# GpSimd drains right behind its last gather, not at the end of the section

## The chip, the cores and the metric

The kernel runs on one core of a Trainium2 chip. The metric is the time of one execution on the device in microseconds, as the median of several executions. Each run also reports the core's span, which here is some 1.7 us shorter than the time; a profile is one recorded execution.

## The reference

An embedding lookup with a position term: 32 batches of 512 indices into a table of 50,000 rows of 512 floats, plus a position row for each place in the sequence.

```python
def reference(indices, embedding_table, position_embed):
    token_embed = embedding_table[indices]
    return (token_embed + position_embed).astype(np.float32)
```

The output is 33.5 MB, and as much is gathered from the table.

## The kernel before

All the work stands in one critical section with hand-written semaphores. GpSimd issues 128 indirect gathers of 128 rows each, VectorE adds the position term to each, and SyncE stores the result.

```python
    with tc.tile_critical():
        # ... SyncE loads the indices and position_embed ...
        for g in range(B * K):                      # 32 * 4 gathers
            # ... waits for the indices and for a free slot ...
            ins = nc.gpsimd.indirect_dma_start(
                out=slots[b % SLOTS][:, k, :], out_offset=None, in_=table,
                in_offset=bass.IndirectOffsetOnAxis(ap=where, axis=0),
            ).then_inc(s_gather[g % LANES], 16)
            if g >= LANES:
                ins._wait_ge(s_gather[g % LANES], rounds(g - LANES))
        # ... TensorE, VectorE, ScalarE ...
        for b, at, n in stores:
            # ... one store, which waits for its adds ...
        nc.sync.wait_ge(s_rest, 16 * rest)          # the last store has landed
```

When the section closes, the built program makes SyncE signal the other engines, each of which executes a drain, by which an engine finishes what it has begun, and answers; SyncE collects the answers. Then come two barriers of all five engines, in which GpSimd counts the others' arrivals and releases them, with three drains of GpSimd around them. Below, "the section's end" is the first part and "the end barrier" the second.

## Time and profile before

| | us |
|---|---|
| time, median of 3 runs | 180.75 (180.0 to 181.29) |
| the profiled execution: time, span | 184.1, 182.4 |
| last packet on the DMA queues | 174.5 |
| from there to the end of the span | 7.9 |

Read the table from the last row up: while the DMA engines are busy, the work is done; after them comes a tail of pure synchronisation. The profiled execution took 3.35 us longer than the median of the timed ones. The lines of the profile are in the prediction. In them SP is SyncE, POOL GpSimd, DVE VectorE, ACT ScalarE and PE TensorE; a q marks an engine's sequencer.

### The profile page before, as it was taken

How to read it: one execution, taken by the hardware profiler on the slowest of the kernel's cores; microseconds unless marked ns; L12 is line 12 of the kernel's file. 1: busy time of each engine (PE TensorE's matmuls, PEld its weight loads, DVE VectorE, ACT ScalarE, POOL GpSimd, SP SyncE). 2: the span in 40 equal slices, each digit the busy share in tenths (PEclk: the TensorE clock that was granted, in tenths of full speed). 3: DMA queues.
4: the chain of work that ended last, by engine and by line, in shares of the span. 5: the costliest groups of instructions: out<-in, count | busy, mean ns of one | idle time of the engine just before them, and what ended most of it. 6: DMA issues, size and time to landing. Idle time of an engine off the chain costs nothing.

```text
span 182.4 us, 398 instructions
## 1 busy us (share of the span) xinstructions
PE 0.7 (0%) x4; PEld 0.6 (0%) x4; DVE 87.1 (48%) x130; ACT 3.6 (2%) x5; POOL 121.8 (67%) x134
## 2 busy tenths in 40 slices
PE   0100000000000000000000000000000000000000
PEld 0100000000000000000000000000000000000000
DVE  0253635546545445738355644455474655454400
ACT  2500000000000000000000000000000000000000
POOL 3777777777777777777777777777777777750000
DMA  4999999999999999999999999999999999999910
GB/s 116 323 270 345 356 382 405 413 405 418 394 371 396 408 403 406 403 417 420 417 413 412 418 412 408 417 418 417 414 412 422 404 415 416 418 407 417 406 70 0
DMA packets 17634, 68.32 MB, mean 375 GB/s; under 512 B 3008, under 2 KB 3008, under 8 KB 14560
## 3 DMA queue, kind: packets, MB, share of 16 engines
q0 software_dynamic: 10240, 33.56, 48.4%
q1 hardware_dynamic: 7392, 34.74, 46.6%
q14 instruction: 2, 0.02, 0.0%
HBM read 34.74 MB, written 33.55 MB: 374 GB/s over the span
## 4 chain that ended last, share of the span: by engine, by line
POOL 63%; issue 24%; DMA 6%; DVE 1%; SPq 0%; POOLq 0%
POOL slot L121 63%; DMA slot<-in_embedding_table_dram,idx_t 5%; DVE slot L150 1%; DMA idx<-in_indices_dram 1%; POOLq L119 0%; SPq L193 0%; SPq L94 0%
## 5 line engine op out<-in xcount | busy, mean ns | idle before, releaser
L121 POOL DMA_INDIRECT slot<-in_embedding_table_dram,idx_t x124 | 117.3, 946 | 37.8 <-issue 37.8
L150 DVE TENSOR_TENSOR slot<-slot,pos_ps 128x512 f32<-128x512 f32 x128 | 86.4, 687 | 80.0 <-issue 39.3
L121 POOL DMA_INDIRECT slot<-in_embedding_table_dram,idx x4 | 4.0, 993 | 2.5 <-DMA idx<-in_indices_dram 1.6
L139 DVE CAST idx_f<-idx_raw 32x512 f32<-32x512 int32 x1 | 0.4, 415 | 4.5 <-DMA idx_raw<-in_indices_dram 4.5
L156 ACT COPY pos_ps<-pos_sb 128x512 f32<-128x512 f32 x4 | 2.3, 587 | 4.4 <-DMA pos_sb<-in_position_embed_dram 4.4
L156 ACT ACT_TABLE_LOAD x1 | 1.3, 1283 | 1.0 <-SPq L94 1.0
L133 PE MATMUL turned<-ident,idx_f 32*128 32x32 f32 x4 | 0.7, 307 | 4.9 <-DVE idx_f L139 4.9
L142 DVE CAST idx_t<-turned 128x128 int32<-128x128 f32 x1 | 0.3, 291 | 0.8 <-PE turned L133 0.8
L133 PEld LDWEIGHTS turned<-ident,idx_f 32*128 32x128 f32 x4 | 0.6, 208 | 4.9 <-DVE idx_f L139 4.9
L106 POOL MEMSET ones<- 32x32 f32 x1 | 0.1, 115 | 0.5 <-SPq L94 0.5
L182 POOL MEMSET const-float32-0.0<- 128x1 f32 x1 | 0.1, 103 | 0.3 <-issue 0.3
L107 POOL TENSOR_SCALAR_AFFINE_SELECT ident<-ones 32x32 f32<-32x32 f32 x1 | 0.2, 203 | 0.1
L182 POOL MEMSET const-uint8-127<- 128x1 uint8 x1 | 0.1, 120 | 0.0
L182 POOL MEMSET const-bfloat16-1.0<- 128x1 bf16 x1 | 0.1, 114 | 0.0
L182 POOL MEMSET const-float32-1.0<- 128x1 f32 x1 | 0.1, 106 | 0.0
## 6 DMA issues: line engine op xcount, KB each, us to landing
out_dram<-slot SPq DMA_DIRECT2D x24, 1024.0 KB
out_dram<-slot SPq DMA_DIRECT2D x10, 512.0 KB
out_dram<-slot SPq DMA_DIRECT2D x12, 256.0 KB
slot<-in_embedding_table_dram,idx_t POOLq DMA_INDIRECT x124
pos_sb<-in_position_embed_dram SPq DMA_DIRECT2D x4, 256.0 KB, 3.0
idx_raw<-in_indices_dram SPq DMA_DIRECT2D x1, 128.0 KB, 3.0
slot<-in_embedding_table_dram,idx POOLq DMA_INDIRECT x4
idx<-in_indices_dram SPq DMA_DIRECT2D x1, 4.0 KB, 1.7
```

The source lines that it names most:

```text
L106: nc.gpsimd.memset(ones[:], 1.0).then_inc(s_ident, 1)
L107: nc.gpsimd.affine_select(out=ident[:], in_=ones[:], pattern=[[-1, B]], compare_op=mybir.AluOpType.is_equal, fill=0.0, base=0, channel_mul ...
L121: ins = nc.gpsimd.indirect_dma_start(out=slots[b % SLOTS][:, k, :], out_offset=None, in_=table, in_offset=bass.IndirectOffsetOnAxis(ap=whe ...
L133: ins = nc.tensor.transpose(turned[:, k, :], idx_f[:, :, k], ident[:])
L139: nc.vector.tensor_copy(out=idx_f[:].rearrange("b p k -> b (p k)"), in_=idx_raw[:, :, 0])._wait_ge(s_raw, 16).then_inc(s_cast, 1)
L142: nc.vector.tensor_copy(out=idx_t[:], in_=turned[:])._wait_ge(s_turn, K).then_inc(s_idx, 1)
L150: nc.vector.tensor_tensor(out=part, in0=part, in1=pos_ps[k][:], op=add)._wait_ge(s_gather[g % LANES], rounds(g)).then_inc(s_add, 1)
L156: nc.scalar.copy(out=pos_ps[k][:], in_=pos_sb[k][:])._wait_ge(s_pos[k], 16).then_inc(s_ps, 1)
L182: nc = _bacc.Bacc("TRN2", target_bir_lowering=False, num_devices=1)
```

## The change

The intent: GpSimd has nothing to do after its last gather, so its drain can be worked off there, beside the last transfers, rather than in the serial tail. A flag takes GpSimd's drain out of the section's end (a nop stands in its place), and a drain is written behind the gathers. On the other engines the built program is the same.

```diff
-    with tc.tile_critical():
+    with tc.tile_critical(no_gpsimd_drain=True):
...
             if g >= LANES:
                 ins._wait_ge(s_gather[g % LANES], rounds(g - LANES))
+        nc.gpsimd.drain()
```

## The prediction

> **What bounds the kernel now.** I read four things in this order: the page for the span and the rows of slices, the stretches of the span for the end, the chain of waits, and then the instructions by source line, because the last stretch holds none that the page counts as busy. The page first:
>
> ```profile
> span 182.4 us, 398 instructions
> ...
> POOL 3777777777777777777777777777777777750000
> DMA  4999999999999999999999999999999999999910
> ```
>
> A slice is 4.56 us. The DMA engines are full from the third slice to the thirty-eighth; GpSimd (POOL) issues its last gather at 162 us; after about 174.5 us nothing moves. The stretches say it more sharply (columns: the stretch, its length, busy us and number of instructions of each engine, granted clock, DMA share, GB/s):
>
> ```profile
> 100.00:140.00 40.00, 0.00 (x0) 0.00 (x0) 21.68 (x33) 0.00 (x0) 30.25 (x33) 1.00 1.02 415
> 165.00:174.60 9.60, 0.00 (x0) 0.00 (x0) 3.44 (x6) 0.00 (x0) 0.00 (x0) 1.00 0.96 386
> 174.60:182.40 7.80, 0.00 (x0) 0.00 (x0) 0.00 (x0) 0.00 (x0) 0.00 (x0) 1.00 0.00 0
> ```
>
> Two parts, then: a body of about 174.6 us bound by DMA bandwidth (share 1.02, 415 GB/s), and a tail of 7.8 us, 4.3% of the span, in which no byte moves and no engine computes. The change can only act on the tail, or on the last 12 us of the body, where GpSimd is idle today. The chain of waits does not help: it follows back from the last busy instruction, an add on VectorE that ends at 172.3 us, and never sees the tail.
>
> ```profile
> POOL 63%; issue 24%; DMA 6%; DVE 1%; SPq 0%; POOLq 0%
> ```
>
> The tail is found by asking for the instructions of the line that opens the critical section (L94), and of the line to which the kernel's end barrier is booked (L193). Rows: line, sequencer, operation, count, duration in ns (min/median/max), first and last start in us:
>
> ```profile
> L94 SPq COMPARE_BRANCH  x1: 33/33/33, 174.9 to 174.9; - x1
> L94 SPq EVENT_SEMAPHORE  x3: 17/713/1397, 175.1 to 177.9; - x3
> L94 SPq NOP  x1: 691/691/691, 179.4 to 179.4; - x1
> L94 ACTq DRAIN  x1: 8/8/8, 175.1 to 175.1; - x1
> L94 POOLq DRAIN  x1: 2515/2515/2515, 175.1 to 175.1; - x1
> L94 DVEq DRAIN  x1: 17/17/17, 175.1 to 175.1; - x1
> L94 PEldq DRAIN  x1: 8/8/8, 175.1 to 175.1; - x1
> ```
>
> ```profile
> L193 POOLq EVENT_SEMAPHORE  x4: 17/17/17, 179.4 to 182.3; - x4
> L193 POOLq DRAIN  x3: 34/34/131, 177.7 to 180.0; - x3
> L193 SPq DRAIN  x3: 4/11/699, 180.7 to 182.2; - x3
> L193 ACTq EVENT_SEMAPHORE  x2: 17/17/17, 179.5 to 182.3; - x2
> ```
>
> SyncE sees the last store land, leaves the section (174.9) and signals the four others. All drain. Three need 8 to 17 ns; GpSimd needs 2515 ns. SyncE collects the five answers, then two barriers follow, at 179.4 and 182.2. The reader is to see that one drain is 150 times as long as any other and stands in the middle of a serial tail.
>
> **What the Trainium skill says.** "Perfetto Trace Analysis", section "Sequencer-only Instruction (DRAIN, etc)": the profiler reports only execution, from the moment the instruction's semaphores are satisfied; waiting is not in the duration. The trace agrees: GpSimd's drain starts at 175.1, with the other engines', so 2515 ns is work, not waiting. "PSUM — Partial Sum Buffer", section "Engine vs sequencer instructions": a drain waits for the engine to go fully idle, while a nop does not wait for work in flight. "VectorE: DVE Perf Modes", section "The DRAIN you can't avoid": boilerplate drains in preamble and postamble are about 12 ns on all five engines. The trace agrees for four engines and disagrees for GpSimd, which alone issued software DMAs. No page says what a GpSimd drain costs behind indirect DMAs; that the 2515 ns belong to the 128 gathers (2515/128, about 20 ns each) is my guess. Every gather had landed by 171.2 us, the end of the last packet of their queue in the trace, 3.9 us before the drain began. So the time is not waiting for data either.
>
> **The change part by part.** The built programs differ by two instructions on GpSimd and by nothing on the other engines.
>
> 1. Added: a plain drain right behind the last gather. The row of gathers puts the last start at 162.0 us and takes 0.946 us, so the drain starts at about 162.9. It has until 175.1, when SyncE signals, so 12.2 us of idle GpSimd. If it only works off finished gathers as they land, it ends just after 171.2. If it first waits for all of them and then needs its full 2.5 us, it ends at 171.2 + 2.5 = 173.7, still 1.4 us early. Cost on the path that sets the end: 0 in both cases.
> 2. Removed: the drain at the section's end. A nop takes its place, waits for the same signal, and gives the same answer. Say 0.03 us, by the small instructions around it. GpSimd then answers at about 175.15 instead of 177.64.
> 3. Kept: the three GpSimd drains of the end barrier. Today they cost 34, 131 and 34 ns, the first straight after the long one. In the changed kernel the first is again a drain with nothing issued since the last one, so I take 34 ns again.
>
> What that is worth depends on whether SyncE really waits for GpSimd. The semaphore updates in the trace say yes: GpSimd's answer is posted at 177.64 and SyncE's next step at 177.67, 0.03 us later, while the other three have answered by 175.2. Gain if SyncE is otherwise prompt: 177.64 - 175.18 = 2.46 us, so 180.75 - 2.46 = 178.3 us, or 1.4%.
>
> **The rivals.**
>
> *SyncE is slow by itself.* Its records in the tail are spaced by multiples of about 0.7 us (1397, 713, 691, 699 ns), and it still works through them until 182.2, long after GpSimd is done. If those steps are real and owe nothing to GpSimd, SyncE reaches the step that needs GpSimd late anyway: three steps of 0.7 us after 175.2 is 177.3, and the gain shrinks to about 0.4 us (180.4). Against it: the first end barrier passes at 179.4 and needs SyncE, yet SyncE's record of arriving there is stamped after 182, so its stamps lag the events and can't be taken literally. Partly for it: SyncE does arrive 1.7 us after GpSimd's answer at the first barrier, and the profiled execution took 184.1 us against 180.75 without a profile, as if the recording itself slowed it. Without recording I expect a prompt SyncE, so a larger share of the 2.46 us.
>
> *The drain's cost reappears later.* If the 2.5 us is not the gathers' bookkeeping but the price of the first drain after a long idle, the first drain of the end barrier pays it: it would run from 175.2 to 177.7, beside SyncE's steps, and hold the barrier instead. Gain 0 to 0.1 us without a profile. For it: nothing but that idle time was not varied. Against it: GpSimd's drain at the kernel's start took 193 ns.
>
> *The early drain disturbs the body.* If it keeps looking at descriptor rings while the last eight or so gathers and stores are moving, it could slow them. The section's last 12 us run at 386 to 413 GB/s; a loss of 5% there would be 0.6 us. Nothing in the profile speaks for it. If the early drain ran beyond 175.1, GpSimd would answer late again; it would have to be 4 us or longer after the last landing to lose anything.
>
> None of these makes the kernel slower by over 2% (3.6 us), and none gains 3.6 us: the whole drain is 2.5.
>
> **Range and chances.** I weigh a full gain (178.3) at 0.7, a small one (180.2) at 0.15, none (180.7) at 0.15: 0.7 x 178.3 + 0.15 x 180.2 + 0.15 x 180.7 = 178.9. The most likely value is lower than the mean; I choose 178.6. The three runs of before spread over 180.0 to 181.29, so 0.7 us either way. Low end: the full gain with a fast run, 177.5. High end: 180.5, a small gain in a usual run. Faster by over 2% needs less than 177.1 us: 0.04. Slower by over 2% needs more than 184.4: 0.01. Within 2%: 0.95.
>
> **What would show it right or wrong.** In the changed profile, step 1 is right if a GpSimd drain starts near 163 us and ends before 175 (its length should be near 8 us if it waits for landings). Step 2 is right if GpSimd shows a short nop near 175.1, and the first barrier comes about 2.4 us earlier relative to the last store. Step 3 is right if the end barrier's first GpSimd drain stays near 34 ns; a 2.5 us drain there means that the cost came back. If SyncE's 0.7 us steps fill the gap, the tail after 174.6 stays near 7.8 us although GpSimd answered early: then SyncE was the limit. If the body's end moves beyond 174.6 us by more than the usual spread, the early drain disturbed the transfers.

## The result, and the profile after

The changed kernel took 178.75 us (median of 4 runs, 178.02 to 179.02), the kernel before 180.6 us (4 runs, 180.0 to 181.29). The ratio is 0.989 with a 95% interval of 0.9843 to 0.9937: some 1% faster. A ratio here is the mean time of one kernel's fast runs over that of the other's of the same rounds, so not quite the ratio of the medians.

The changed kernel's page, the two rows that answer to those shown of before:

```profile
span 177.0 us, 399 instructions
...
POOL 4777777777777777777777777777777777776000
DMA  4989999999999999999999999999999999999993
```

The DMA row is now full up to the last slice. The empty slices at the end are gone. The stretches of the end:

```profile
165.00:175.00 10.00, 0.00 (x0) 0.00 (x0) 3.91 (x6) 0.00 (x0) 0.00 (x0) 1.00 0.93 376
175.00:177.00 2.00, 0.00 (x0) 0.00 (x0) 0.00 (x0) 0.00 (x0) 0.00 (x0) 1.00 0.00 0
```

The tail without a moving byte is 2.0 us instead of 7.8. That is 5.8 us less, far more than the drain's 2.5 us and than the 1.9 us by which the medians differ. So these two profiles must not be subtracted from each other. First the rows of the section's end and of the end barrier (which is now booked to line 194), then the early drain (line 129):

```profile
L94 SPq EVENT_SEMAPHORE  x3: 17/28/28, 175.6 to 175.9; - x3
L94 POOLq NOP  x1: 13/13/13, 175.7 to 175.7; - x1
L94 SPq NOP  x1: 13/13/13, 175.9 to 175.9; - x1
```

```profile
L194 POOLq EVENT_SEMAPHORE  x4: 17/17/17, 176.1 to 176.9; - x4
L194 POOLq DRAIN  x3: 34/41/131, 175.7 to 176.7; - x3
L194 SPq DRAIN  x3: 7/7/7, 176.0 to 176.3; - x3
```

```profile
L129 POOLq DRAIN  x1: 23301/23301/23301, 150.2 to 150.2; - x1
```

Two things have changed. GpSimd's drain is out of the tail: 23.3 us long, it ends at 173.5, and a nop of 13 ns answers in its place. And SyncE is quick: its steps take 7 to 28 ns, where in the profile of before most took 700 to 1400. The change can't be the plain cause of the second, as SyncE executes the same instructions.

The difference between the two recordings is visible in part 6 of the page, the issues with the time to landing. Before, and after:

```profile
slot<-in_embedding_table_dram,idx_t POOLq DMA_INDIRECT x124
```

```profile
slot<-in_embedding_table_dram,idx_t POOLq DMA_INDIRECT x124, 8.0
```

A landing time is printed only where the trace has all the semaphore updates of a transfer. The trace of before holds 760 updates, that of after 3384. From 40 us to 160 us, the former has 172, one per 0.70 us on average, and the latter 2003. 0.70 us is also the step that SyncE shows in the tail of before. I call the two kinds a sparse and a full recording. The experiments had to find out whether the kind belongs to the kernel or to where it runs, and what the change is worth in each.

### The profile page after: what moved, and what is told of

Its sections match the earlier page's. It is cut to its first block, busy times and chain, and to the rows that moved or that the text cites. A ratio compares the mean times of both kernels' runs of the same rounds, so it can differ in the third digit from the quotient of the medians.

```text
span 177.0 us, 399 instructions
## 1 busy us (share of the span) xinstructions
PE 0.7 (0%) x4; PEld 0.6 (0%) x4; DVE 87.7 (50%) x130; ACT 3.6 (2%) x5; POOL 122.1 (69%) x134
## 4 chain that ended last, share of the span: by engine, by line
POOL 65%; issue 25%; DMA 7%; POOLq 1%; DVE 0%; SPq 0%
POOL slot L121 65%; DMA slot<-in_embedding_table_dram,idx_t 6%; DMA idx<-in_indices_dram 1%; POOLq L129 1%; DVE slot L151 0%; SPq L194 0%; POOLq L119 0%; SPq L94 0%
```

## The experiments

### One chip, the change and its halves

Four kernels ran on one chip: the kernel before again (e1), the flag alone (e2), the early drain alone (e3), and the whole change again (e4).

```diff
 e2: flag only
-    with tc.tile_critical():
+    with tc.tile_critical(no_gpsimd_drain=True):
 e3: early drain only
+        nc.gpsimd.drain()          # behind the last gather; the section keeps its own
```

> The kernel before, unchanged, profiled a second time. All theories: GpSimd's drain at the end of the section is again about 2.5 us, and starts within 0.1 us of the other engines' drains. If SyncE's steps of 0.7 us in the tail belong to the long GpSimd drain, they come again and the profiled span is again about 182; if they were a whim of that one recording, SyncE takes under 0.1 us a step and the span is near 179, with a tail after the last store of about 4.0 us (1.5 us as in the changed kernel, plus 2.5).

> Only half of the change: the drain at the section's end is off, no drain behind the last gather. My theory (the cost is GpSimd's bookkeeping of the gathers and must be paid once, by the first drain that follows): the first drain of the end barrier takes 2.5 us in place of 0.04, starts near 175.7 and holds the first barrier; SyncE reaches that barrier 0.4 us after the section's end, so all but 0.4 us of the cost stays: ratio to before 0.998, about 180.2 us. Rival (taking the drain out of the section is what helps, the early one is decoration): ratio 0.987 to 0.989 as for the whole change.

> The other half: a drain behind the last gather, and the section's own drain kept. My theory: the early drain pays, the later one finds nothing to do and takes about 0.04 us; ratio 0.987 to 0.990, as the whole change. Rival (a drain after long idle costs 2.5 us whatever was drained before): the section's drain is 2.5 us again and the ratio is 1.00.

> The changed kernel, unchanged, in five rounds for a narrower interval and a second profile. Full gain of 2.46 us would be a ratio of 0.986; the first measurement gave 0.989. If the early drain disturbs the last gathers, the last store lands later than in the kernel before by some 0.5 us on the same chip; if not, the landing times agree within 0.3 us and the ratio tends to 0.986.

| kernel | median us | ratio to before (95%) | span of the profiled run |
|---|---|---|---|
| before (9 runs beside them) | 184.18 (184.07 to 184.33) | | |
| e1, before again | 184.2 (one look) | | 182.5 |
| e2, flag only | 184.24 | 0.9994 (0.998 to 1.0008) | 182.5 |
| e3, early drain only | 184.26 | 1.0005 (0.9991 to 1.0018) | 182.4 |
| e4, the change | 184.19 | 0.9993 (0.9979 to 1.0007) | 182.5 |

On this chip the kernel before took 184.2 us in every run, as in its first profile, and the change was worth nothing. All four recordings are sparse (754 to 770 updates). So the kind doesn't go with the kernel: the changed kernel, full in its first profile, is sparse here. Whether it goes with the chip or with the time of the run isn't shown: this was one session on one chip, and the later ones, all full, were three sessions on two other chips (the chip of the first profiles isn't on record). The rows of e4 at the section's end and of its end barrier:

```profile
L94 SPq EVENT_SEMAPHORE  x3: 17/1398/1398, 175.4 to 178.7; - x3
L94 POOLq NOP  x1: 13/13/13, 175.5 to 175.5; - x1
L94 SPq NOP  x1: 697/697/697, 180.1 to 180.1; - x1
```

```profile
L194 POOLq EVENT_SEMAPHORE  x4: 17/17/17, 180.2 to 182.4; - x4
```

GpSimd has answered at 175.5, and its early drain (22.2 us, ended at 172.8) is done. Still SyncE walks in steps of 0.7 us, the first barrier passes at 180.2 and the second near 182.3. The freed time is filled by the slow SyncE. In e1 SyncE does wait for the drain, as the prediction read it: GpSimd's answer is posted at 177.97 and SyncE's next step at 178.00. Yet the first barrier passes at 180.2 in e1 as in e4, whether the answer came early or late. In e2 the drain's 2.5 us moved into the end barrier (176.1 to 178.6), in e3 it was worked off early; neither shows in the time. In all five sparse traces, of before and of e1 to e4, the update of SyncE's arrival at the last barrier stands between 182.15 and 182.31, though SyncE left the section anywhere from 174.8 to 175.8. It is as if something held SyncE up to a fixed moment.

My expectations for e2, e3 and e4 missed the time on this chip. So did the guess in e1 that the steps of 0.7 us might belong to the long drain: e4 has them without it. What the traces show of GpSimd's drain is as expected in all three.

### The same four with the tail moved to a later time

If the hold-up ends near 182.2, a tail that starts later should be clean on any chip. The pad is four adds on VectorE, on buffers whose stores have landed, between the last landing and the section's end. The results stay correct.

```diff
-        nc.sync.wait_ge(s_rest, 16 * rest)
+        for i in range(4):
+            pad = nc.vector.tensor_tensor(
+                out=slots[8 + i][:], in0=slots[12][:], in1=slots[13][:], op=add)
+            if i == 0:
+                pad._wait_ge(s_rest, 16 * rest)
+            if i == 3:
+                pad.then_inc(s_pad, 1)
+        nc.sync.wait_ge(s_pad, 1)
```

> The kernel before with a pad: after the last store has landed, four adds of 128x2048 on VectorE (each about four times the 0.69 us of a 128x512 add, so 9 to 11 us in all), and only then the end of the section. Reason: on the last chip every kernel ended at 182.4, and in those traces only one semaphore update was recorded per 0.71 us, against a full record in the first profile of the changed kernel; SyncE stepped at the same 0.70 us until 182.2 whatever GpSimd did. Theory A (a held-up recording slows SyncE up to a fixed time near 182.2, and hides GpSimd's drain): the padded tail starts after 184 and is clean: about 0.3 + 2.5 + 1.3 us from the end of the last pad to the end of the span, GpSimd's drain 2.5 us. Theory B (SyncE is slow in every tail on such a chip, wherever it stands): the tail again takes 7 to 8 us with steps of 0.7 us. On a chip with full records both theories give the clean tail.

> The changed kernel with the same pad. Theory A: clean tail of about 1.5 us; 2.3 to 2.5 us shorter than the padded kernel before on the same chip, whichever kind of chip it is. Theory B: no difference on a chip with sparse records.

> Only the section's own drain taken out, with the pad. Theory A with the cost paid by the first later drain: the end barrier's first GpSimd drain takes 2.5 us, as it did without the pad; the end comes 0.3 to 0.5 us earlier than in the padded kernel before, not 2.4. Theory B: no difference on a chip with sparse records.

> Only the early drain added, the section's own kept, with the pad. Theory A: the section's drain takes 0.04 us, the time is within 0.1 us of the padded changed kernel. Theory B: no difference on a chip with sparse records.

| kernel, padded | median us (5 runs) | pad's end to span's end, us |
|---|---|---|
| p1, before | 189.41 (189.13 to 189.53) | 183.90 to 187.72: 3.82 |
| p2, the change | 187.04 (187.0 to 187.87) | 183.75 to 185.30: 1.55 |
| p3, flag only | 189.19 (189.09 to 189.56) | 184.08 to 187.84: 3.75 |
| p4, early drain only | 187.15 (187.04 to 187.7) | 184.00 to 185.55: 1.55 |

This was another chip, with full recordings (3386 to 3388 updates) and the kernel before at 180.73 us. So it doesn't decide between theories A and B. It does take the change apart cleanly. p1, p2, p3 and p4, the rows at the section's end (line 95 in the padded kernels) and the end barrier's drains:

```profile
L95 POOLq DRAIN  x1: 2515/2515/2515, 184.1 to 184.1; - x1
L95 SPq NOP  x1: 13/13/13, 186.7 to 186.7; - x1
```

```profile
L95 POOLq NOP  x1: 13/13/13, 184.0 to 184.0; - x1
L95 SPq NOP  x1: 13/13/13, 184.2 to 184.2; - x1
```

```profile
L95 POOLq NOP  x1: 13/13/13, 184.3 to 184.3; - x1
...
L202 POOLq DRAIN  x3: 40/123/2515, 184.4 to 187.6; - x3
```

```profile
L95 POOLq DRAIN  x1: 41/41/41, 184.2 to 184.2; - x1
```

The SPq NOP is the step that needs GpSimd's answer. In p1 it comes 2.7 us after SyncE has left the section at 183.93, right behind the drain; in p2 0.5 us after 183.78. In p3 the drain isn't gone: the first drain of the end barrier pays the full 2515 ns. So the flag alone saves 3.82 - 3.75 = 0.07 us of tail (0.22 us by the medians; I had expected 0.3 to 0.5), and the early drain alone (p4) saves as much as the whole change, 2.27 us, because the section's own drain then takes 41 ns. The early drain is the change; the flag is nearly decoration. The whole change is worth 189.41 - 187.04 = 2.37 us here, by the medians.

The four also answer whether the early drain disturbs the last transfers. The last store landed at 174.83 and 175.08 us with it (p2, p4), at 174.98 and 175.17 without (p1, p3). No disturbance shows.

### What the 2515 ns are

First, whether they are the price of waking an idle engine. One small memset on GpSimd goes in front of the drain of p1:

```diff
+        nc.gpsimd.wait_ge(s_ident, 2)
+        nc.gpsimd.wait_ge(s_pad, 1)
+        nc.gpsimd.memset(ones[:], 1.0)
```

> The padded kernel before, with one small memset on GpSimd right before the section's end, after the pad, so that GpSimd has been woken 0.3 us before its drain. If the 2515 ns are the gathers' bookkeeping, the drain stays at 2.4 to 2.5 us. If they are the price of a first instruction after a long idle, the memset or the time around it takes them and the drain falls below 0.3 us. Besides, if this chip records sparsely: a held-up recording up to a fixed time (theory A) gives a clean padded tail with SyncE steps under 0.1 us; SyncE slow in every tail (theory B) gives steps of 0.7 us after 184.

The section's drain:

```profile
L95 POOLq DRAIN  x1: 2533/2533/2533, 183.8 to 183.8; - x1
```

The memset took 115 ns, its usual length, from 0.1 us before the drain's start to 10 ns after it, and the drain still took 2533 ns. p4 says the same from the other side: there GpSimd was idle for 11 us behind its early drain, and the section's drain took 41 ns. Idle time is not the cause.

Second, whether the cost goes with the number of gathers since the last drain. A drain is put between two gathers of p1, so that fewer are left for the section's own.

```diff
         for g in range(B * K):
+            if g == 64:              # 112 and 32 in the other two runs
+                nc.gpsimd.drain()
```

> The padded kernel before, with one more drain in the middle, between the 64th and the 65th gather; the section's own drain stays. Bookkeeping per gather: 64 gathers are left for the last drain, so 1.26 us in place of 2.5. A flat price of a drain behind any gathers: 2.5 us again. The drain in the middle holds back the issue until everything issued has landed, so the body grows by 5 to 12 us: a price of draining at the wrong place. Theories A and B as in the run beside it.

> As the run with a drain after 64 gathers, but after 112, so that 16 are left for the section's drain. There, 64 left cost 5281 ns, more than the 2515 ns of 128 gathers with no drain between, so the cost isn't 20 ns per gather. New theory: the drain works off the gathers that GpSimd has not yet retired, at 5281/64 = 83 ns each, and while it issues, GpSimd retires old ones by itself when it must, so that some 30 were left after 128. Then 16 left cost 1.3 us. Rival (a drain's cost doubles or adds a fixed amount with each earlier real drain, whatever is left): about 5.3 us again. If this chip records sparsely: theory A a clean padded tail, theory B SyncE steps of 0.7 us after 184.

> The same with the drain after 32 gathers, 96 left. The new theory at 83 ns each: 7.9 us if none of the 96 has been retired by then, less if GpSimd has had to retire some (then the number tells how many). Rival: about 5.3 us again.

The section's drain with 64, 16 and 96 gathers left:

```profile
L95 POOLq DRAIN  x1: 5281/5281/5281, 193.0 to 193.0; - x1
```

```profile
L95 POOLq DRAIN  x1: 1361/1361/1361, 194.4 to 194.4; - x1
```

```profile
L95 POOLq DRAIN  x1: 7894/7894/7894, 191.4 to 191.4; - x1
```

With 64 left the drain took twice as long as with all 128: my first guess of 20 ns per gather fell here. The three points lie on a line: (5281 - 1361)/48 = 81.7 ns and (7894 - 5281)/32 = 81.7 ns per gather, with 54 ns left over at zero, near the 34 to 46 ns of a drain with nothing to do. The second theory had been put down as 1.3 and 7.9 us before the last two runs, and both came out; its rival had put 5.3 us for each. By the same line, the 2515 ns of the kernel before are (2515 - 54)/81.7 = 30 gathers. The other 98 must have been settled while GpSimd was still issuing; this is inferred from the number, not shown.

The same three traces hold the drain in the middle as well. Like that of the change, it begins with gathers still under way (after 64, 112 and 32 gathers):

```profile
L119 POOLq DRAIN  x1: 22853/22853/22853, 69.1 to 69.1; - x1
```

```profile
L119 POOLq DRAIN  x1: 25022/25022/25022, 130.0 to 130.0; - x1
```

```profile
L119 POOLq DRAIN  x1: 21392/21392/21392, 28.0 to 28.0; - x1
```

By the semaphore updates, the last gather before each had landed at 89.29, 150.37 and 48.05 us, and the drain ended 2.66, 4.62 and 1.35 us later. Half of 54 ns + 81.7 ns per gather is 2.64, 4.60 and 1.33 us. The change fits too: its drain ends 1.27 us after the last landing, and half of 2515 ns is 1.26. So in all six traces with a drain that began early and landing times, half of what a late drain costs was left when the last gather landed. Why half isn't shown.

This also narrows down the 98. By this half, the drain after 112 gathers still had work for all 112, so whatever settled the others came between the 113th gather and the last. GpSimd's records don't show it: in the kernel before, no gather but the first took over 955 ns, and no pause between two was over 0.31 us, while 98 gathers at 81.7 ns would be 8.0 us (an estimate from the line above).

A drain at the wrong place is dear. These kernels took 201.1, 198.5 and 202.1 us (one execution each) against 189.2 for p5 on the same chip. Part of this is the longer drain at the section's end; the section itself ended 9.2, 10.5 and 7.5 us later than in p5, within the 5 to 12 us expected of the first. In the row of slices of the run with the drain after 64 gathers, GpSimd stops and the DMA share sags:

```profile
POOL 4777777777777777503777777777777777400000
DMA  4899999999999999996789999999999999997000
```

From the start of one gather to the start of the next it is 10.6 us there, 13.9 us with the drain after 112 and 8.1 us after 32, where 1.25 us is usual. A drain in the middle holds back all later gathers until the earlier ones have landed and the drain has done the rest of its work: the 64th landed at 89.29, the drain ended at 91.95, and the 65th started at 92.68.

### What stays open

On the one chip that recorded sparsely, every kernel took 183.6 to 184.3 us, and the change gained nothing; where recordings were full, the kernel before took 180.0 to 181.3 us and the change gained 1%. SyncE isn't slow all through a sparse run. In all five, each of its 46 stores starts within 29 ns of the add that it waits for, as in the full ones, and after the arrival near 182.2 its last steps take 3 to 17 ns. That SyncE is slow in between because its own records wait for a held-up recording is supported by this, by the common step of 0.70 us and by the common end near 182.2, but not shown: no padded kernel met such a recording, so theory B (SyncE slow in every tail there) isn't excluded. The timed runs list spans too, so they may be recorded in the same way; what either kernel takes without any recording isn't known.

## Why the prediction was right

The time was predicted as 178.6 us with a range of 177.5 to 180.5, and measured as 178.75, within 2% as forecast. Part of this is luck. The 2.46 us were read from a sparse profile and taken off a time of the full kind, and the change was then timed where recordings are full. On the chip of e1 to e4 it gave 184.19 against 184.18, outside the range. The 178.6 itself is a choice between the full gain (178.3) and the weighted mean (178.9). What the drain costs, and that SyncE waits for it, was right. By its steps:

- **Step 1, the early drain is hidden: right.** It ended at 173.5, 1.9 us before SyncE left the section at 175.46. The prediction saw two cases: it ends with the last landing, or a full 2.5 us later. It came halfway: 1.27 us after the last gather's landing in each of the three traces that show that landing (after, p2, p4). The landing itself was misread: 171.2 is the end of the last packet, while the add that waits for this gather starts at 171.6 in before (in after, packet 171.77, landing 172.25). Its record looked otherwise than foretold: it starts at 150.2 and not near 163. The Trainium skill's "Perfetto Trace Analysis", section "Sequencer Loop", says why this can be: the sequencer pushes engine instructions into a queue and goes on, while a control instruction starts executing in it. The trace agrees: the last gather started only at 162.2, 12 us after the drain's record had begun. So a drain's window can contain waiting for earlier gathers. The prediction's "work, not waiting" took more from its page than the wait for semaphores that the page speaks of; for the 2515 ns it holds because all gathers had landed before.
- **Step 2, a nop answers in place of the drain: right in kind, and 0.2 us too large in size.** The nop took 13 ns, in p3 too, where the drain's 2515 ns were still to be paid: it waits for none of that work. The gain was put at 2.46 us, from the other engines' answers at 175.18. But SyncE does not stand ready then: in p2 it reaches the step that needs GpSimd at 184.25, 0.27 us after GpSimd's nop at 183.98. That part of the drain was hidden already. The tails of p1 and p2 differ by 2.27 us.
- **Step 3, the end barrier's drain stays short: right.** 41 ns against 34.
- **The rival of a slow SyncE: true where recordings are sparse.** The prediction argued from a lag of SyncE's stamps, and expected a prompt SyncE "without recording". The first half stands: in the trace of e1, GpSimd's count completes at 180.2, before SyncE's own arrival is stamped. But the timed runs are slow too on the chip of e1 to e4, so it isn't the profiled execution as such. The kernel before had been profiled in one state and timed in the other, and the 3.35 us between 184.1 and 180.75 was the sign of it.
- **The rival of a cost that reappears: wrong for the change, right for half of it.** With the early drain in place nothing reappears. With the flag alone all of it does (p3), but not for the reason that the rival gave, a long idle: p5 and p4 exclude that.
- **The guess of 20 ns per gather** was wrong: 81.7 ns for each gather not yet settled, of which some 30 were left. The time didn't rest on it.
- **Three readings that went too far, without effect on the gain.** "150 times as long as any other" holds among the drains of the section's end alone: the lines beside it show drains of 131 ns (GpSimd) and 699 ns (SyncE). The DMA row is full from the second slice, not the third. And "bound by DMA bandwidth" isn't shown for the body: the DMA share is 1.02, but GpSimd too issues one gather per 1.25 us without a pause over 0.31 us, and the chain shown gives it and its pauses (POOL and issue) 87% of the span. The change touches neither.

No run beat the changed kernel; the tail that is left, 1.55 us in p2, is the end of the section and the two barriers: many steps of a few tens of ns, and on GpSimd a drain of 123 ns and a clearing of semaphores of 269 ns.

## What to carry to other kernels

Look behind the last busy instruction: the chain of waits ends there, and a serial tail of drains and barriers can follow that only the rows by source line show. A drain that must be paid once is free where its engine has finished and others still work, and dear where later work of the same engine waits behind it. Leave it room: here half of it was still to do after the last landing, and 3.2 us were left until SyncE went on. Before two profiles are subtracted, check that both are of the same kind, by the time of the profiled run against the timed ones and by whether landing times are there at all.

## What the Trainium skill lacked or had wrong

- "VectorE: DVE Perf Modes", section "The DRAIN you can't avoid", gives boilerplate drains as about 12 ns on all five engines. In the full recordings the drains of four engines agree (7 to 17 ns). GpSimd's don't: 192 to 196 ns at the kernel's start, 2515 ns at the section's end behind 128 indirect gathers, 34 to 46 ns straight after another drain, and 123 to 131 ns for the second of the end barrier. Whether the section's drains are among those that the page means isn't shown.
- No page says what a GpSimd drain costs behind indirect DMAs. Here: 54 ns plus 81.7 ns for each of 16, 64 and 96 gathers issued since the last drain, long after all had landed; 2515 ns for 128 with no drain between; and when it starts early, half of this is left after the last landing (1.27 us behind 128 gathers; 1.35, 2.66 and 4.62 us behind 32, 64 and 112).
- "Perfetto Trace Analysis", section "Sequencer-only Instruction (DRAIN, etc)", has the reported window start when the semaphores are satisfied, and names no other wait. A drain without a semaphore wait, queued behind gathers, spends its window waiting for them: 23.3 us from 150.2, where the engine began its last gather only at 162.2.
- No page puts a number to how one kernel's recordings and times can differ from one chip or session to another: 754 to 770 recorded semaphore updates against 3384 to 3388, steps of SyncE in the tail of mostly 0.70 us or its double against 7 to 28 ns, and 184.2 us against 180.7 us for the same kernel.
